# Delta-rule stage of a hybrid layer: GpSimd's two-tensor operations on other engines, and one convolution over context and tokens

## The chip, the core and the metric

The kernel runs on one core of a Trainium2 chip. A core has five engines that run side by side and meet at semaphores: PE (matrix products), DVE (VectorE, elementwise), ACT (ScalarE, function and copy), POOL (GpSimd) and SP, which issues DMAs. Each engine works its own instructions strictly in the order of the program. The metric is the device time of one execution in microseconds (us), as the median of repeated runs.

## The reference

One layer takes 512 latent tokens and 256 context tokens of width 1024. After modulated RMS norm, one projection feeds a bidirectional gated delta rule (8 heads of 128) and a latent attention (8 heads); their outputs are gated, merged, projected and followed by a squared-ReLU MLP. The change concerns the delta rule:

```python
def _centred_conv(x, w):                       # width 5, along the tokens; context and latents apart
    k_w = w.shape[0]; t = x.shape[1]; p = k_w // 2
    xp = jnp.pad(x, ((0, 0), (p, p), (0, 0)))
    return sum(xp[:, i:i + t] * w[i] for i in range(k_w))
# _gdn_inputs: qkv = silu(conv(qkv)); q, k = l2norm(q), l2norm(k); beta = sigmoid(..); g = -exp(a) * softplus(..)
a_mat = jnp.where(strict, einsum(kb, k) * decay, 0.0)
t_mat = triangular_solve(eye + a_mat, eye, lower=True, unit_diagonal=True)
u, w = t_mat @ vb, t_mat @ (kb * exp(gc))
def step(s, inp):                              # over the chunks, forwards and backwards
    v_new = u_i - w_i @ s
    o_i = qd_i @ s + qk_i @ v_new
    s = s * gl_i + kd_i.T @ v_new
```

## The kernel before, in words

Work is laid out with 128 rows on the partitions. The 256 context tokens are blocks 0 and 1, the 512 latent tokens blocks 2 to 5 of 128. Products run as three products of high and low parts (`mm3`), so each weight chunk that comes by DMA as `wf` is split by `wchunk` into `wh` (a cast on ScalarE, L180) and `wl` (a subtraction `wf - wh`, L181, on the engine `eng`). For the chunks of `w_qkv` (24 chunks of two pieces), `w_z` (8) and `w_gate` (16) `eng` is GpSimd, 96 pieces of 128x512 in all; elsewhere it is VectorE, or both in turn.

The delta rule takes two heads at a time (a pair), four pairs. For each pair:

- `gdn_in` projects k, v and q of both heads into PSUM. `convolve` copies each result to `raw` (ScalarE, L459), scales it by the middle tap (ScalarE, L461) and adds the four other taps on VectorE (L465), for the 512 latent columns and for the 256 context columns apart, then applies silu by a tanh on ScalarE (L469) and one VectorE instruction (L470).
- `gdn_gram` makes decays and Gram matrices for three double blocks. Four instructions of VectorE write the factor `Bt` (L571), GpSimd multiplies it by the decay `gam` (L573), VectorE by the Gram matrix in PSUM into `A` (L579). GpSimd cuts the triangles `rh` that feed the decay products (L555).
- `gdn_prep` inverts the 32x32 diagonal blocks by a loop of 60 dependent VectorE instructions on `pt` and `tu` (L614, L615; called the solve here), with a trip through DRAM before it (`dA`) and behind it (`dB`), and puts the blocks together by products with `off`, which is `A` masked by GpSimd to the neighbours of the diagonal blocks of 32 and then of 64 (L606), and with `S`, `S2`, `R`, `R2` (L635 to L653), three of whose products per pair are GpSimd's.
- `gdn_chain` walks the six blocks in both directions. Each step waits for the step before: `Em` and `Qm` (triangles, GpSimd, L710), `rho` (VectorE, L741), products, `y2` (VectorE, two instructions per direction, L756), `y` (ScalarE, L761), products, the state `s` (VectorE, L777).
- `gdn_out` norms and gates the output (`ob`, VectorE, L822).

The chunks of `w_z` and `w_gate` are written at low priority between pairs, to fill TensorE. The order on each engine is not written by hand: the program is given to a scheduler that fixes each engine's order before the run, from its own idea of how long things take. Two lines set what is done at one time:

```python
    prep1 = gdn_prep(1, ops1, gram1)
    ops2, gram2 = gdn_in(2)
    with low():
        fill(1)
    gdn_out(1, gdn_chain(1, ops1, prep1))
```

so the solve of one pair lies beside the projections and convolutions of the next and the chain of the one before. Latent attention and the MLP follow.

Of the kernel before, what the change touches and what calls it, by code (L numbers as in the profile page):

```python
# [7 lines left out]
F32 = mybir.dt.float32  # L8
# [7 lines left out]
P = 128  # L16
# [18 lines left out]
def _masks():  # L35
# [16 lines left out]
        "off32": (p // 64 == i // 64) & (p // 32 != i // 32),  # L52
        "off64": p // 64 != i // 64,
# [32 lines left out]
def tile_layer(ctx, tc, I, out, stop=None, dbg=None):  # L86
# [123 lines left out]
    def gemv_step(q, acc, kt, ws):  # L210
        """acc += silu(c) * rows of w_mod."""
# [46 lines left out]
    def spill(piece, b, po, tag):  # L258
        """normalised rows, transposed, to DRAM."""
# [24 lines left out]
    def rms(t, n, r, tag):  # L284
        """1 / rms over the channels, in every partition."""
# [128 lines left out]
    # rotated key part, shared by the heads  # L414
# [38 lines left out]
    def convolve(pl, pc, ch, dst, nctx):  # L453
        """dst (P, nctx + 512) = silu(conv)."""
        raw = gx.tile([P, NT], F32, tag="raw", name="raw")
        for src, o, L in ((pl, nctx, NL), (pc, 0, NC)):
            if src is None:
                continue
            act.copy(raw[:, o:o + L], src)  # L459
            src = raw[:, o:o + L]  # L460
            act.activation(dst[:, o:o + L], src, AF.Identity, scale=convh[:, ch, 2:3])  # L461
            for i in (0, 1, 3, 4):
                s = i - 2
                a, z = max(0, -s), L - max(0, s)
                dve.scalar_tensor_tensor(dst[:, o + a:o + z], src[:, a + s:z + s], convh[:, ch, i:i + 1],  # L465
                                         dst[:, o + a:o + z], ALU.mult, ALU.add)
        n = nctx + NL
        tt = raw[:, :n]
        act.activation(tt, dst, AF.Tanh)  # L469
        dve.scalar_tensor_tensor(dst, tt, 1.0, dst, ALU.add, ALU.mult)  # L470

    def transposes(src, nb, tag):
        """src (P, nb*128) -> list of (PSUM tile, first block, count)."""
        res = []
        b = 0
        while b < nb:
# [880 lines left out]
```

## Time and profile before

| | us |
|---|---|
| median of three executions | 1366.33 |
| the three executions | 1363.82, 1366.33, 1374.16 |
| profiled execution, span from the first to the last instruction | 1372.9 |
| busy in that span: PE, DVE, ACT, POOL | 1286.1, 907.8, 614.5, 423.8 |
| DVE busy from 125 to 640 us (delta rule) | 391 |

The profile's span is that of one execution; what lies around it is not in its rows. A busy PE counts overlapped ends of matmuls and is not PE at its peak. Of each group of instructions the profile gives busy time, mean length, and the idle time before it with what ended it. [...]

### The profile page before, as it was taken

To read this page: it belongs to the slowest core of one execution; us is meant where nothing else is said; L and a number is where in the kernel's file an instruction comes from. 1 tells how busy PE (TensorE), PEld (TensorE's weight loads), DVE (VectorE), ACT (ScalarE), POOL (GpSimd) and SP (SyncE) were. 2 spreads that over 40 slices of the span, in tenths; PEclk is the share of its full clock that TensorE was granted. 3 is DMA by queue.
4 is the path that set the end of the run, shared out by engine and by line. 5 is a ranking of instruction groups with operands and counts; after the bars stand their busy time and mean duration, and the time that the engine had idled before them with its cause. 6 is when DMAs were issued, how large, how long until landed. Compare 5 with 4: busy or idle time off the path is not lost.

```text
span 1372.9 us, 21048 instructions
## 1 busy us (share of the span) xinstructions
PE 1286.1 (94%) x7430; PEld 1124.4 (82%) x7430; DVE 907.8 (66%) x1925; ACT 614.5 (45%) x1562; POOL 423.8 (31%) x446
## 2 busy tenths in 40 slices
PE   5999887998998989898999999999999999999998
PEld 4897776797787978787888998888897888888887
DVE  4758798777877787846886887786877333333333
ACT  4555544336452635335565776523353233242331
POOL 0156557443653564441222221122123011010110
PEclk9999998999999999998999999999999999999999
DMA  9332213320233123324010101485734222222232
GB/s 365 99 121 80 56 54 91 94 70 1 93 109 92 31 78 109 100 84 145 7 51 12 38 32 69 167 300 164 267 112 165 88 98 93 100 93 99 93 104 96
DMA packets 97992, 141.33 MB, mean 103 GB/s; under 512 B 32736, under 2 KB 41824, under 8 KB 97760
## 3 DMA queue, kind: packets, MB, share of 16 engines
q1 hardware_dynamic: 68576, 127.41, 27.4%
q10 hardware_dynamic: 29312, 12.59, 3.7%
q8 instruction: 59, 0.97, 0.3%
q14 instruction: 45, 0.37, 0.1%
HBM read 124.36 MB, written 15.60 MB: 102 GB/s over the span
## 4 chain that ended last, share of the span: by engine, by line
PE 57%; DVE 15%; ACT 4%; DMA 3%; issue 2%; POOL 1%; ACTq 0%; SPq 0%; DVEq 0%; POOLq 0%
PE d L186 14%; PE d L188 13%; PE d L187 13%; DVE tu L614 2%; DVE vT L465 2%; DVE pt L615 2%; PE c L749 1%; PE p L1028 1%; PE c L734 1%; PE p L186 1%; PE p L187 1%; PE p L188 1%; PE c L769 1%; DVE pp L1018 1%; PE p L657 1%
## 5 line engine op out<-in xcount | busy, mean ns | idle before, releaser
L180 ACT CAST wh<-wf 128x512 fp32r<-128x512 f32 (+2 forms) x292 | 176.8, 610 | 382.3 <-PE d L187 260.6
L181 POOL TENSOR_TENSOR wl<-wf,wh 128x512 fp32r<-128x512 f32 x120 | 168.3, 1403 | 271.8 <-ACT wh L180 253.7
L181 DVE TENSOR_TENSOR wl<-wf,wh 128x512 fp32r<-128x512 f32 (+2 forms) x172 | 115.6, 677 | 121.0 <-ACT wh L180 119.8
L186 PE MATMUL d<-hTh,wh 128*128 128x512 f32 x384 | 158.7, 413 | 1.2 <-DVE tz L839 1.1
L187 PE MATMUL d<-hTl,wh 128*128 128x512 f32 x384 | 156.6, 408 | 0.0
L188 PE MATMUL d<-hTh,wl 128*128 128x512 f32 x384 | 155.6, 407 | 0.0
L1215 POOL TENSOR_TENSOR a<-r 128x512 f32<-128x512 f32 (+1 forms) x36 | 36.4, 1012 | 271.3 <-ACT r L1213 264.7
L186 PE MATMUL d<-ah,wh 128*128 128x512 f32 x256 | 100.7, 395 | 0.0
L187 PE MATMUL d<-al,wh 128*128 128x512 f32 x256 | 100.7, 395 | 0.0
L188 PE MATMUL d<-ah,wl 128*128 128x512 f32 x256 | 100.6, 395 | 0.0
L188 PE MATMUL d<-h2h,wl 128*128 128x512 f32 x224 | 87.4, 390 | 2.4 <-DVE wl L181 2.4
L186 PEld LDWEIGHTS d<-hTh,wh 128*128 128x128 f32 x384 | 75.6, 197 | 16.1 <-DVE tz L839 1.7
L188 PEld LDWEIGHTS d<-hTh,wl 128*128 128x128 f32 x384 | 75.3, 196 | 14.9
L187 PE MATMUL d<-h2l,wh 128*128 128x512 f32 x224 | 87.2, 389 | 0.0
L186 PE MATMUL d<-h2h,wh 128*128 128x512 f32 x224 | 87.2, 389 | 0.0
L187 PEld LDWEIGHTS d<-hTl,wh 128*128 128x128 f32 x384 | 75.5, 197 | 13.8
L1254 DVE SCALAR_TENSOR_TENSOR x<-d,mcol,x 128x512 f32<-128x512 f32 x32 | 24.0, 751 | 61.5 <-PE d L188 61.5
L614 DVE TENSOR_TENSOR tu<-pt 96x30 f32<-96x30 f32 (+14 forms) x120 | 52.9, 441 | 17.7 <-DMA pt<-dA 14.9
L188 PEld LDWEIGHTS d<-ah,wl 128*128 128x128 f32 x256 | 48.1, 188 | 11.6
L186 PEld LDWEIGHTS d<-ah,wh 128*128 128x128 f32 x256 | 48.1, 188 | 11.5
L187 PEld LDWEIGHTS d<-al,wh 128*128 128x128 f32 x256 | 48.1, 188 | 11.5
L615 DVE TENSOR_TENSOR pt<-pt,tu 96x30 f32<-96x30 f32 (+14 forms) x120 | 53.1, 442 | 2.8
(544 smaller groups left out, 3531.0 us busy)
## 6 DMA issues: line engine op xcount, KB each, us to landing
wf<-in_w_mi SPq DMA_DIRECT2D x64, 256.0 KB, 2.6
wf<-in_w_mo SPq DMA_DIRECT2D x64, 256.0 KB, 2.6
wf<-in_w_qkv SPq DMA_DIRECT2D x48, 256.0 KB, 2.7
wm<-in_w_mod SPq DMA_DIRECT2D x40, 256.0 KB, 5.4
wm<-in_w_mod SPq DMA_DIRECT2D x16, 512.0 KB, 9.1
wf<-in_w_gate SPq DMA_DIRECT2D x32, 256.0 KB, 2.6
wms<-in_w_mod SPq DMA_DIRECT2D x12, 512.0 KB, 8.2
wf<-in_w_z SPq DMA_DIRECT2D x16, 256.0 KB, 2.7
```

The source lines that it names most:

```text
L180: act.copy(wh, wf)
L181: eng.tensor_tensor(wl, wf, f32(wh), ALU.subtract)
L186: pe.matmul(po, lh, rh, start=first, stop=False)
L187: pe.matmul(po, lh, rl, start=False, stop=False)
L188: pe.matmul(po, ll, rh, start=False, stop=last)
L465: dve.scalar_tensor_tensor(dst[:, o + a:o + z], src[:, a + s:z + s], convh[:, ch, i:i + 1], dst[:, o + a:o + z], ALU.mult, ALU.add)
L614: dve.tensor_tensor(o, bc(pt[:, 0:k, k:k + 1], [96, k, w]), bc(pt[:, k:k + 1, k + 1:], [96, k, w]), ALU.mult)
L615: dve.tensor_tensor(pt[:, 0:k, k + 1:], pt[:, 0:k, k + 1:], o, ALU.add)
L657: pe.matmul(pv[:, c, :], off[:, c, :], R[:, c, :], start=True, stop=True)
L734: pe.matmul(t[:, 0, h, :], kT[:, h, 128 * bs[d]:128 * bs[d] + 128], S_[d][:, h, :], start=True, stop=True)
L1215: pool.tensor_tensor(a_, r, r, ALU.mult)
L1254: dve.scalar_tensor_tensor(x1[:, ot, :], po, mcol[:, 5, ot, 0:1], x1[:, ot, :], ALU.mult, ALU.add)
```

## The change

The code of the delta-rule stage is altered at these places; attention and MLP are as before but for the shape of one buffer.

- `wl` of `w_qkv`, `w_z` and `w_gate` is made by VectorE: 96 instructions change engine.
- `Bt` is written by ScalarE (48 instructions with a scale and a bias from memory), and its product with `gam` is VectorE's (12).
- The three products of `Dc` with the masks "up", "s2" and "s" are VectorE's (12).
- `off` is one lasting buffer. Instead of products with masks (24), GpSimd sets blocks to zero and copies blocks of `A`: per pair 2 memsets of 64 partitions, 4 copies of 32 partitions, 4 memsets of 32 partitions, 2 copies of 64.
- Of the two `y2` instructions of a step and direction one goes to ScalarE (40 of 80); the scaling of `ob` goes to ScalarE (32).
- `raw` is one lasting buffer with two zero columns before, between and behind context and tokens, so that each tap of k and v is one instruction over 770 columns, not two over about 512 and 256 (64 in place of 128), and ScalarE's scaling is one too. As the tanh overwrites the columns between, GpSimd sets them to zero again after each of the 16 convolutions. q keeps its 512 columns.

```diff
-    def convolve(pl, pc, ch, dst, nctx):
-        raw = gx.tile([P, NT], F32, tag="raw", name="raw")
-        for src, o, L in ((pl, nctx, NL), (pc, 0, NC)):
-            if src is None:
-                continue
-            act.copy(raw[:, o:o + L], src)
-            src = raw[:, o:o + L]
-            act.activation(dst[:, o:o + L], src, AF.Identity, scale=convh[:, ch, 2:3])
-            for i in (0, 1, 3, 4):
-                s = i - 2
-                a, z = max(0, -s), L - max(0, s)
-                dve.scalar_tensor_tensor(dst[:, o + a:o + z], src[:, a + s:z + s], convh[:, ch, i:i + 1],
-                                         dst[:, o + a:o + z], ALU.mult, ALU.add)
-        n = nctx + NL
-        tt = raw[:, :n]
+    GAP = 2
+    NG = NT + GAP
+    raw = gx.tile([P, NG + 2 * GAP], F32, name="raw")
+    pool.memset(raw[:, 0:GAP], 0.0)
+    pool.memset(raw[:, GAP + NC:GAP + NC + GAP], 0.0)
+    pool.memset(raw[:, NG + GAP:], 0.0)
+    def at(b):
+        return 128 * b + (GAP if b >= 2 else 0)
+    def convolve(pl, pc, ch, dst):
+        o = 0 if pc is not None else NC + GAP
+        n = NG - o
+        act.copy(raw[:, GAP + NC + GAP:GAP + NG], pl)
+        if pc is not None:
+            act.copy(raw[:, GAP:GAP + NC], pc)
+        act.activation(dst, raw[:, o + 2:o + 2 + n], AF.Identity, scale=convh[:, ch, 2:3])
+        for i in (0, 1, 3, 4):
+            dve.scalar_tensor_tensor(dst, raw[:, o + i:o + i + n], convh[:, ch, i:i + 1], dst, ALU.mult, ALU.add)
+        tt = raw[:, o + 2:o + 2 + n]
         act.activation(tt, dst, AF.Tanh)
         dve.scalar_tensor_tensor(dst, tt, 1.0, dst, ALU.add, ALU.mult)
+        if pc is not None:
+            pool.memset(raw[:, GAP + NC:GAP + NC + GAP], 0.0)
...
-            pl, pc = project(wchunk(I["w_qkv"][8 + hd], eng=pool), True)
+            pl, pc = project(wchunk(I["w_qkv"][8 + hd]), True)
...
+    off = gy.tile([P, 12, P], F32, name="off")
+    for c0 in range(0, 12, 4):
+        pool.memset(off[:, c0:c0 + 4, :], 0.0)
...
-                    dve.tensor_scalar(Bt[:, 2 * bb + h, :], f32(maskr[:, 1, :]), sA[:, b, 0, h:h + 1], sA[:, b, 1, h:h + 1],
-                                      op0=ALU.mult, op1=ALU.add)
-            pool.tensor_tensor(Bt, Bt, gam, ALU.mult)
+                    act.activation(Bt[:, 2 * bb + h, :], f32(maskr[:, 1, :]), AF.Identity,
+                                   scale=sA[:, b, 0, h:h + 1], bias=sA[:, b, 1, h:h + 1])
+            dve.tensor_tensor(Bt, Bt, gam, ALU.mult)
...
-        def masked(m):
-            t = gy.tile([P, 12, P], F32, tag="off", name="off")
-            for b2 in range(3):
-                cs = slice(4 * b2, 4 * b2 + 4)
-                pool.tensor_tensor(t[:, cs, :], A[:, cs, :], bc(M(m).unsqueeze(1), [P, 4, P]), ALU.mult)
-            return t
-        off = masked("off32")
+        def neighbours(n, fill):
+            for d in range(P // n):
+                q = slice(n * d, n * d + n)
+                e = slice(n * (d ^ 1), n * (d ^ 1) + n)
+                if fill:
+                    pool.tensor_copy(off[q, :, e], A[q, :, e])
+                else:
+                    pool.memset(off[q, :, e], 0.0)
+        neighbours(64, False)
+        neighbours(32, True)
...
-        pool.tensor_tensor(Dc, Dc, bc(M("up").unsqueeze(1), [P, 12, 32]), ALU.mult)
+        dve.tensor_tensor(Dc, Dc, bc(M("up").unsqueeze(1), [P, 12, 32]), ALU.mult)
...
-        expand(pool, S2, Dc)
+        expand(dve, S2, Dc)
         S = Dc
-        pool.tensor_tensor(S, Dc, bc(M("s").unsqueeze(1), [P, 12, 32]), ALU.mult)
+        dve.tensor_tensor(S, Dc, bc(M("s").unsqueeze(1), [P, 12, 32]), ALU.mult)
...
-        off2 = masked("off64")
+        neighbours(32, False)
+        neighbours(64, True)
...
-                    for h in HH:
-                        dve.tensor_scalar(t[:, h, :], p2[d][:, 0, h, :], bkd[:, bs[d], d, h:h + 1], None, op0=ALU.mult)
+                    dve.tensor_scalar(t[:, 0, :], p2[d][:, 0, 0, :], bkd[:, bs[d], d, 0:1], None, op0=ALU.mult)
+                    act.activation(t[:, 1, :], p2[d][:, 0, 1, :], AF.Copy, scale=bkd[:, bs[d], d, 1:2])
...
-                dve.tensor_scalar(ob[:, h, b, :], ob[:, h, b, :], so[:, h, b:b + 1], None, op0=ALU.mult)
+                act.activation(ob[:, h, b, :], ob[:, h, b, :], AF.Copy, scale=so[:, h, b:b + 1])
...
-        pz, _ = project(wchunk(I["w_gate"][i], eng=pool), False)
+        pz, _ = project(wchunk(I["w_gate"][i]), False)
...
-        pz, _ = project(wchunk(I["w_z"][hd], eng=pool), False)
+        pz, _ = project(wchunk(I["w_z"][hd]), False)
```

The scheduler then fixes another order. On VectorE, in the solve of the first pair, the rows before were these (`tu` and `pt` are the solve, `kT`, `vT` the convolution of the next pair):

```order
L614 TENSOR_TENSOR tu<-pt 96x234
L465 SCALAR_TENSOR_TENSOR vT<-raw,convh,vT 128x511
L465 SCALAR_TENSOR_TENSOR vT<-raw,convh,vT 128x254
L615 TENSOR_TENSOR pt<-pt,tu 96x18x13
L465 SCALAR_TENSOR_TENSOR vT<-raw,convh,vT 128x511
L465 SCALAR_TENSOR_TENSOR vT<-raw,convh,vT 128x255
L614 TENSOR_TENSOR tu<-pt 96x238
L465 SCALAR_TENSOR_TENSOR vT<-raw,convh,vT 128x510
L465 SCALAR_TENSOR_TENSOR vT<-raw,convh,vT 128x255
L615 TENSOR_TENSOR pt<-pt,tu 96x17x14
```

and at the same step of the solve they now are these (L629 and L630 are the solve, L474 ends a convolution, `br` are scalars of the next pair):

```order
L629 TENSOR_TENSOR tu<-pt 96x234
L510 TENSOR_SCALAR ssk<-ssk 128x6
L179 TENSOR_TENSOR wl<-wf,wh 128x512
L630 TENSOR_TENSOR pt<-pt,tu 96x18x13
L512 RECIPROCAL r_1916<-ssk 128x6
L474 SCALAR_TENSOR_TENSOR vT<-raw,vT 128x770
L629 TENSOR_TENSOR tu<-pt 96x238
L548 TENSOR_TENSOR br_2100<-beta,r_1916 128x24
L630 TENSOR_TENSOR pt<-pt,tu 96x17x14
L179 TENSOR_TENSOR wl<-wf,wh 128x512
```

The split convolution rows have moved away from this step, and two `wl` now stand between dependent rows of the solve.

On GpSimd, where the first pair's Gram matrices begin (`nk` is a power of six columns, `rh` triangles), the rows before were

```order
L181 TENSOR_TENSOR wl<-wf,wh 128x512
L151 TENSOR_TENSOR nk<-ssk,expt 128x6
L181 TENSOR_TENSOR wl<-wf,wh 128x512
L151 TENSOR_TENSOR nk<-ssk,expt 128x6
L181 TENSOR_TENSOR wl<-wf,wh 128x512
L573 TENSOR_TENSOR Bt<-Bt,gam 128x512
L181 TENSOR_TENSOR wl<-wf,wh 128x512
L606 TENSOR_TENSOR off<-A,mk 128x512
```

and now

```order
L149 TENSOR_TENSOR nk<-ssk,expt 128x6
L476 MEMSET raw 128x2
L536 MEMSET off 128x512 x3
L621 MEMSET off 64x12x64 x2
L149 TENSOR_TENSOR nk<-ssk,expt 128x6
L476 MEMSET raw 128x2
L566 AFFINE_SELECT rh<-ghi 128x256
L566 AFFINE_SELECT rh<-glo 128x256
L566 AFFINE_SELECT rh<-ghi 128x256
```

The `wl`, the product of `Bt` and the masked `off` are gone from here; memsets of `raw` and `off` stand in their place.

Later on GpSimd, where the first pair's blocks are put together and its chain begins (`Em`), the rows before were

```order
L573 TENSOR_TENSOR Bt<-Bt,QK 128x512
L647 TENSOR_TENSOR S_1831<-D_1801,mk 128x768
L181 TENSOR_TENSOR wl<-wf,wh 128x512 x2
L653 TENSOR_TENSOR D_1801<-D_1801,mk 128x384
L606 TENSOR_TENSOR off<-A,mk 128x512 x3
L181 TENSOR_TENSOR wl<-wf,wh 128x512 x5
L606 TENSOR_TENSOR off<-A,mk 128x512 x3
L181 TENSOR_TENSOR wl<-wf,wh 128x512
L710 AFFINE_SELECT Em<-A 128x256 x2
```

and now

```order
L631 MEMSET pt 96x32
L566 AFFINE_SELECT rh<-glo 128x256
L621 MEMSET off 32x12x32 x4
L619 COPY off<-A 64x12x64 x2
L621 MEMSET off 64x12x64 x2
L619 COPY off<-A 32x12x32 x4
L727 AFFINE_SELECT Em<-A 128x256 x4
```

Between the end of the solve and the first `Em`, memsets and copies stand where products and `wl` stood.

## Rows read from the trace of the kernel before

**Rows 1.** Windows of the delta-rule stage: busy us (instructions) per engine, granted clock, DMA.

```profile
core 0 of [0], span 1372.9 us
core 0: us, PE busy (x) PEld busy (x) DVE busy (x) ACT busy (x) POOL busy (x), PEclk, DMA share, GB/s
125.00:250.00 125.00, 105.36 (x560) 89.98 (x558) 101.13 (x180) 61.66 (x159) 78.96 (x82) 0.92 0.28 77
250.00:370.00 120.00, 109.97 (x709) 98.64 (x708) 98.98 (x228) 52.31 (x141) 59.19 (x72) 0.94 0.19 58
370.00:490.00 120.00, 116.23 (x706) 104.09 (x707) 91.90 (x217) 58.40 (x161) 60.85 (x69) 0.95 0.26 73
490.00:640.00 150.00, 135.67 (x746) 118.00 (x745) 99.31 (x221) 59.71 (x150) 67.23 (x75) 0.92 0.36 109
```

**Rows 2.** Chain that ended last, 259 to 640 us: share by line; then start, us, piece.

```profile
by line: PE d L186 6.9%; DVE tu L614 6.8%; DVE vT L465 6.8%; PE d L187 6.7%; PE d L188 6.7%; DVE pt L615 6.6%; issue 3.2%; PE c L749 2.8%; PE p L657 2.4%; DMA D<-dB 2.3%; PE c L734 2.3%; PE c L769 2.1%; PE p L691 2.0%; DMA dA<-DTa 1.9%; DMA
...
485.83 2.06 POOL Bt L573
```

**Rows 3.** Timeline of DVE and POOL, the third pair's solve: start us, us, engine, line.

```profile
401.02 0.96 DVE L614 TENSOR_TENSOR tu<-pt 96x30 f32<-96x30 f32 x1 [5.06 <-DMA pt<-dA]
...
407.36 0.55 POOL L710 TENSOR_SCALAR_AFFINE_SELECT Qm<-QK 128x256 f32<-128x256 f32 x1 [1.61 <-PE e L788]
407.68 0.43 DVE L614 TENSOR_TENSOR tu<-pt 96x184 f32<-96x184 f32 x1
408.15 0.34 DVE L615 TENSOR_TENSOR pt<-pt,tu 96x184 f32<-96x184 f32 x1
...
418.74 0.40 DVE L614 TENSOR_TENSOR tu<-pt 96x238 f32<-96x238 f32 x1
418.76 1.54 POOL L181 TENSOR_TENSOR wl<-wf,wh 128x512 fp32r<-128x512 f32 x1 [4.59 <-PE c L769]
419.18 1.39 DVE L615 TENSOR_TENSOR pt<-pt,tu 96x238 f32<-96x238 f32 x1
...
432.96 0.19 DVE L615 TENSOR_TENSOR pt<-pt,tu 96x30 f32<-96x30 f32 x1
```

**Rows 4.** One group of POOL, whole span: count | busy us, mean ns | idle before.

```profile
L181 POOL TENSOR_TENSOR wl<-wf,wh 128x512 fp32r<-128x512 f32 x120 | 168.3, 1403 | 271.8 <-ACT wh L180 253.7 <-PE c L769 7.0 <-issue 4.7
```

**Rows 5.** Groups of DVE, whole span, same columns.

```profile
L181 DVE TENSOR_TENSOR wl<-wf,wh 128x512 fp32r<-128x512 f32 (+2 forms) x172 | 115.6, 677 | 121.0 <-ACT wh L180 119.8 <-PE d L187 0.7
L614 DVE TENSOR_TENSOR tu<-pt 96x30 f32<-96x30 f32 (+14 forms) x120 | 52.9, 441 | 17.7 <-DMA pt<-dA 14.9
L615 DVE TENSOR_TENSOR pt<-pt,tu 96x30 f32<-96x30 f32 (+14 forms) x120 | 53.1, 442 | 2.8
L465 DVE SCALAR_TENSOR_TENSOR vT<-raw,convh,vT 128x510 f32<-128x510 f32 (+3 forms) x64 | 49.5, 814 | 4.0 <-ACT vT L461 3.7
L465 DVE SCALAR_TENSOR_TENSOR kT<-raw,convh,kT 128x510 f32<-128x510 f32 (+3 forms) x64 | 40.2, 671 | 9.4 <-ACT kT L461 9.0
L465 DVE SCALAR_TENSOR_TENSOR qT<-raw,convh,qT 128x510 f32<-128x510 f32 (+1 forms) x32 | 30.2, 944 | 7.5 <-ACT qT L461 7.0
L571 DVE TENSOR_SCALAR Bt<-maskr,sA 128x128 f32<-128x128 f32 x48 | 26.4, 613 | 0.1
L822 DVE TENSOR_SCALAR ob<-ob,so 128x128 f32<-128x128 f32 x32 | 11.8, 436 | 2.5 <-POOL so L151 2.3
L756 DVE TENSOR_SCALAR y<-c,bkd 128x128 f32<-128x128 f32 x80 | 23.7, 341 | 12.9 <-PE c L749 12.7
```

**Rows 6.** One line of DVE: count, ns min/median/max, first and last start.

```profile
L470 DVE SCALAR_TENSOR_TENSOR kT<-raw,kT x8: 943/958/1399, 96.8 to 471.2; 128x768 f32<-128x768 f32 x8
```

**Rows 7.** Groups of ACT, whole span, columns as in rows 4.

```profile
L761 ACT ACTIVATE y<-c,br 128x128 f32<-128x128 f32 x64 | 19.9, 367 | 40.7 <-DVE y L756 28.2 <-PE c L749 11.4 <-DMA dA<-DTa 0.9
L523 ACT ACTIVATE junk<-t 128x128 f32<-128x128 f32 x32 | 8.8, 276 | 2.6 <-PE t L480 1.1 <-ACT junk L523 0.5 <-ACT Da L586 0.4
```

**Rows 8.** Waits of POOL, 125 to 640 us: us in total, times, longest.

```profile
POOL wl L181 <- ACT wh L180: 97.0, 45, 7.9
```

More of the change, by code (lines that the diff above doesn't have):

```diff
@@ L479, in transposes @@
             for q in range(n):
-                pe.transpose(t[:, 128 * q:128 * q + 128], src[:, 128 * (b + q):128 * (b + q) + 128], ident)
+                c = at(b + q) if nb == 6 else 128 * (b + q)
+                pe.transpose(t[:, 128 * q:128 * q + 128], src[:, c:c + 128], ident)
             res.append((t, b, n))
@@ L485, in gdn_in @@
     def gdn_in(pr):
-        kT = gp.tile([P, 2, NT], F32, tag="kT", name="kT", bufs=2)
+        kT = gp.tile([P, 2, NG], F32, tag="kT", name="kT", bufs=2)
         qT = gp.tile([P, 2, NL], F32, tag="qT", name="qT", bufs=2)
@@ L496, in gdn_in @@
             hd = 2 * pr + h
-            pl, pc = project(wchunk(I["w_qkv"][8 + hd], eng=pool), True)
-            convolve(pl, pc, 8 + hd, kT[:, h, :], NC)
+            pl, pc = project(wchunk(I["w_qkv"][8 + hd]), True)
+            convolve(pl, pc, 8 + hd, kT[:, h, :])
             for t, b, n in transposes(kT[:, h, :], 6, "t"):
@@ L509, in gdn_in @@
             hd = 2 * pr + h
-            vT = gx.tile([P, NT], F32, tag="vT", name="vT")
-            pl, pc = project(wchunk(I["w_qkv"][16 + hd], eng=pool), True)
-            convolve(pl, pc, 16 + hd, vT, NC)
+            vT = gx.tile([P, NG], F32, tag="vT", name="vT")
+            pl, pc = project(wchunk(I["w_qkv"][16 + hd]), True)
+            convolve(pl, pc, 16 + hd, vT)
             for t, b, n in transposes(vT, 6, "t"):
@@ L518, in gdn_in @@
             hd = 2 * pr + h
-            pl, _ = project(wchunk(I["w_qkv"][hd], eng=pool), False)
-            convolve(pl, None, hd, qT[:, h, :], 0)
+            pl, _ = project(wchunk(I["w_qkv"][hd]), False)
+            convolve(pl, None, hd, qT[:, h, :])
             for t, b, n in transposes(qT[:, h, :], 4, "t"):
@@ L576, in gdn_gram @@
                 for h in range(2):
-                    s = kT[:, h, 128 * (2 * b2 + bb):128 * (2 * b2 + bb) + 128]
+                    s = kT[:, h, at(2 * b2 + bb):at(2 * b2 + bb) + 128]
                     pe.matmul(v4(pk)[:, 2 * bb + h, :], s, s, start=True, stop=True)
@@ L627, in gdn_prep @@
                     s = 128 * (2 * b2 + bb)
-                    pe.matmul(v4(pq)[:, 2 * bb + h, :], kT[:, h, s:s + 128], qT[:, h, s - NC:s - NC + 128],
+                    ks = at(2 * b2 + bb)
+                    pe.matmul(v4(pq)[:, 2 * bb + h, :], kT[:, h, ks:ks + 128], qT[:, h, s - NC:s - NC + 128],
                               start=True, stop=True)
@@ L680, in gdn_prep @@
         for c in range(12):
-            pe.matmul(pv2[c // 8][:, c % 8, :], off2[:, c, :], R2[:, c].rearrange("p e b -> p (e b)"),
+            pe.matmul(pv2[c // 8][:, c % 8, :], off[:, c, :], R2[:, c].rearrange("p e b -> p (e b)"),
                       start=True, stop=True)
@@ L733, in gdn_chain @@
                     for h in HH:
-                        pe.matmul(t[:, 0, h, :], kT[:, h, 128 * bs[d]:128 * bs[d] + 128], S_[d][:, h, :],
+                        pe.matmul(t[:, 0, h, :], kT[:, h, at(bs[d]):at(bs[d]) + 128], S_[d][:, h, :],
                                   start=True, stop=True)
@@ L1002, in attention @@
         for q2 in range(2):
-            pth = gp.tile([P, 6, 256], F32R, tag="kT", name="pth", bufs=2)
+            pth = gp.tile([P, 2 * NG], F32R, tag="kT", name="pth", bufs=2)[:, 0:1536]
+            pth = pth.rearrange("p (a b) -> p a b", a=6)
             ptl = gp.tile([P, 6, 256], F32R, tag="kn", name="ptl", bufs=2)
```

2 lines of the change are left out of this document (removed).

## The prediction

> **What bounds the kernel now.** I read the windows by stage first. [...] No engine is full, so I read the chain of waits next. From 259 to 640 us the three rows of `d` (TensorE's projections) hold 20.3% of it, and three VectorE rows alone (the two lines of the solve and the convolution of v) 20.2%, which is 77 us of 381 [rows 2]. The stage is a loop that passes through VectorE again and again, with GpSimd in it at places (a product `Bt` of 2.06 us [rows 2]).
>
> Then I looked at why VectorE's instructions are long, in the timeline of a solve. The reader is to see one pattern: the row `pt` of 238 columns starts at 419.18, while GpSimd's `wl` runs from 418.76 to 420.30, and takes 1.39 us; the equally wide row ahead of it, which began just ahead of that `wl`, takes 0.40 [rows 3]. A VectorE instruction with two tensors in SBUF is held until GpSimd's two-tensor instruction ends. GpSimd's triangle `Qm` (one tensor), 0.55 us from 407.36, leaves the first row of 184 columns at 0.43 where the next one, clear of it, takes 0.34 [rows 3]: a one-tensor instruction holds little.
>
> **The change part by part,** in VectorE's time within the stage.
>
> *Onto VectorE.* 96 `wl` at 0.68 [rows 5] are 65 us; 12 products of `Bt`, also 128x512, are 8; 12 products of 384 or 768 columns at about the same length are 8 (5 if all were as short as 0.4, 19 if all were as long as the 1.6 us of a held one). Sum +81.
>
> *Off VectorE.* The 48 rows of `Bt` (L571) were 26.4 us; of `ob` (L822), 11.8, three pairs of four fall in the stage, 9; of `y2` (L756), 23.7, half go, 12 [rows 5]. Sum -47.
>
> *Convolution.* k and v cost 40.2 + 49.5 = 90 us in 128 instructions [rows 5]. Now they are 64 of 770 columns; the nearest row is the 128x768 one of L470 with 0.94 at least and 0.96 in the median [rows 6], so I take 1.0 each, 64 us: -26, between -25 and -30. q keeps its 32 instructions, but their mean of 0.94 [rows 5] is as long as 768 columns take unheld, so they are held by 0.2 or more: -6.
>
> *Solves.* The four solves cost 53 + 53 = 106 us [rows 5]. The third one's 60 rows, the first and the last of them in [rows 3], sum to 24.9 us; six of them are held, two of which [rows 3] shows (0.96 and 1.39 us), and at their neighbours' length it would be 20.3. Four such solves are 81: -25. The same relief on the other two-tensor rows (L470 has 1.40 at most against 0.94 [rows 6]) I put at -4.
>
> *Copies.* 24 block copies read SBUF on GpSimd still. The trace has no copy there. If one holds like `Qm`, 0.1 us, they cost 2; if like `wl`, 1.0, they cost 24. They read one tensor, so I lean to the first, 0.3 each: +7. Memsets read nothing, and I put them at nothing; the time they need on GpSimd is covered by its 249 idle us of the stage [rows 1].
>
> Together 81 - 47 - 26 - 6 - 25 - 4 + 7 = -20 us of 391. The reader should note how little of this comes from the largest move: `wl` on VectorE costs 65 us, against holds of at most its 1.40 us on GpSimd [rows 4], which struck only where a two-tensor row met it. The gain is in the 47 that ScalarE takes and in the merged convolution.
>
> *Path alone.* `Bt` on the chain was four VectorE rows of 0.61 [rows 5] and a GpSimd product, 2.06 where it shows on the chain [rows 2]. On ScalarE a row with one scale from memory takes 0.367 and one without 0.276 [rows 7], so each such operand is 0.09 and `Bt` with two is 0.46: 4 x 0.46 + 0.68 = 2.5 against 4.5, 2 us for each of 12 blocks; I count a quarter on the path, -6. `y2` was two VectorE rows in line, 0.68; now one of 0.34 lies beside one of 0.37: 0.3 for each of 40, half on the path's side, half of those hidden, -3.
>
> *ScalarE* gains 48 x 0.46 + 32 x 0.37 + 40 x 0.37 = 49 us, less about 5 for the merged scaling: 232 to 276 of 515. Not a bound; what it costs, if its cover goes, is in the rivals.
>
> [...]
>
> [...]
>
> *The new queue.* On GpSimd, `wl` waited 97.0 us in 45 waits for ScalarE's cast [rows 8], with little behind it but triangles. Now these waits stand in VectorE's queue, and behind each stand the rows of a solve, a convolution or a chain, as the order shows. VectorE comes to a `wl` later than GpSimd did, so most of the 97 is over by then. I take 6 us, between 0 and 48.
>
> Sum on the path: -20 - 6 - 3 - 5 + 6 = -28 us. Here I take the 20, which is 88 added against 108 removed, as lying on the path wholly: solve and convolution, where the relief falls, are what the chain names most of VectorE [rows 2], and the `wl` stand between their rows. If both counted by VectorE's visible fifth of the chain, the 20 would be 4 (rival 2); if the relief counted wholly and half of the `wl` fitted into idle time, it would be 53 (rival 3). The profiled execution's span is 1372.9 us, 6.6 above the median of 1366.3, and would become 1345; the median becomes 1338.
>
> Attention and MLP, behind 640 us, keep their engines; the last `gdn_out` moves its 3 us there to ScalarE, and the rest is unchanged.
>
> **The rivals.**
>
> 1. *The queue takes it back* (slower). Mechanism: VectorE stands at a `wl` whose `wh` is not cast, because ScalarE, with 44 us more to do, is late, or because the buffer that the cast needs is still read by TensorE; the solve behind it stands too, TensorE then waits for the solve, and the next cast is later still. For: 97 us of such waits were there [rows 8], and 1 to 2 `wl` stand between dependent rows of the solve. Against: ScalarE has 283 idle us in the stage. Each of the 96 needs 0.29 us of waiting in front of the path to cancel the 28, and 0.44 to make the kernel 1% slower (42 us). With half of the 97 the sum is -34 + 48 = +14, 1380 us; with all of it, 1429.
>
> 2. *Nothing to be measured.* The relief falls where VectorE had slack, the added 81 us where the chain runs, and TensorE's filler chunks were covering the waits anyway. For: GpSimd's `wl` cost nothing wherever VectorE read PSUM or idled, and VectorE idles 124 us in the stage [rows 1]. By a fifth of it on the path, -20 becomes -4 and the sum -12: 1354, within 1%.
>
> 3. *More than the sum.* The scheduler knew nothing of the holds, so the order before fell behind its plan, and TensorE's idle time grew with it. [...] With half of the 65 us of `wl` in VectorE's idle time, it is 33 better, 1305. Against: the low-priority chunks are only 48 of the 96.
>
> 4. *The copies hold as long as `wl` did,* so that the change doesn't do what it says. Then 17 us are lost from the sum: 1355, which lies between the forecast and rival 2; I count it with rival 2.
>
> **How the numbers follow.** About 1%, 14 us, is what a measurement of this kernel can tell from no change. The forecast, 1318 to 1352, has 0.46. Rival 3, below 1318, 0.19, of which 0.09 lies below 1300. Rivals 2 and 4, 1353 to 1380, 0.22. Rival 1, above 1380, 0.13. So faster by over 1% is 0.46 + 0.19 = 0.65, within 1% 0.22, slower 0.13. The range goes from 1300 to 1376: it leaves out 0.09 below and some 0.14 above at most, of which the edge of rival 2 is a part, and reaches to the other cases for the rest. The likeliest case's own range is 1318 to 1352.
>
> **What would show each step.** In the profile after: `wl` of 128x512 on VectorE at 0.68 to 0.72, with no row of the solve above 0.6 but beside GpSimd's triangles and copies; the solve's two lines together at 80 to 88 us instead of 106; the 770-column rows at 0.96 to 1.02; `Bt` on ScalarE at 0.42 to 0.50; GpSimd's busy time in the stage under 150 us; VectorE's busy time from 125 us to the end of the stage at 360 to 380. The clock of the stage should rise to 0.95 or more. Rival 1 would show as VectorE's idle time in front of `wl`, put down to ScalarE's cast, of more than 30 us in the stage; rival 2 as VectorE's busy time down by 20 and its idle time up by as much; rival 4 as rows of the solve of 1 us beside copies. The forecast is wrong if VectorE's busy time in the stage does not fall, or if it falls and the stage still ends after 630 us.

## The result and the profile after

The changed kernel takes 1330.53 us in the median (1323.24 to 1335.15), the kernel before 1366.83 beside it: a ratio of 0.972, 95% interval 0.968 to 0.976. The forecast was 1338, with a range of 1300 to 1376. The total was near; the experiments show that it was near for a reason other than the sum's.

The profiled executions are 1372.9 and 1330.7 us long, 42.2 apart. The row of ScalarE that reads latent attention's first projection (`junk`, L930 before, L947 after) stands at 641.8 us before and at 606.4 after, so 35 of the 42 us lie ahead of it, in the delta-rule stage; most of the other 7 in attention, beside which the last pair's chain still runs; the MLP is as long as it was.

The windows of the stage after, the rows that answer to [rows 1] (columns as there, from 125 us to the end of the stage):

```profile
core 0: us, PE busy (x) PEld busy (x) DVE busy (x) ACT busy (x) POOL busy (x), PEclk, DMA share, GB/s
125.00:250.00 125.00, 116.42 (x620) 98.95 (x619) 102.94 (x199) 71.80 (x182) 41.38 (x60) 0.96 0.33 90
250.00:370.00 120.00, 110.99 (x726) 100.50 (x725) 87.08 (x193) 62.97 (x175) 40.41 (x72) 0.94 0.17 49
370.00:490.00 120.00, 117.89 (x740) 105.05 (x740) 93.98 (x211) 70.59 (x196) 34.81 (x57) 0.99 0.30 87
490.00:605.00 115.00, 110.88 (x643) 97.86 (x642) 79.72 (x197) 56.51 (x149) 20.15 (x36) 0.96 0.42 123
```

VectorE is busy 103 + 87 + 94 + 80 = 364 us (391 before), ScalarE 262 (232), GpSimd 137 (266), and the granted clock is 0.94 to 0.99 (0.92 to 0.95). TensorE is busy 456 of 480 us, before 467 of 515.

The chain of waits from 259 to 605 us, by line, against [rows 2]:

```profile
by line: PE d L184 15.9%; PE d L185 15.4%; PE d L186 15.1%; PE c L766 4.1%; PE c L786 3.8%; PE c L751 3.4%; PE e L802 3.3%; PE e L805 2.9%; DVE kT L471 2.0%; issue 1.9%; PE t L487 1.8%; PE p L683 1.7%; DMA sz<-d_z 1.7%; PE p L708 1.6%; PE p
```

TensorE's projections (`d`) had 20.3% and now have 46.4%; the solve's two lines and the convolution of v, which had 20.2%, are gone from the head of the list. Most of the chain is now TensorE's.

The groups of VectorE, ScalarE and GpSimd that answer to [rows 4 to 7], columns as there:

```profile
L179 DVE TENSOR_TENSOR wl<-wf,wh 128x512 fp32r<-128x512 f32 (+2 forms) x268 | 182.9, 686 | 164.2 <-ACT wh L178 161.5 <-PE d L186 1.4 <-PE d L185 0.7
L630 DVE TENSOR_TENSOR pt<-pt,tu 96x30 f32<-96x30 f32 (+14 forms) x120 | 41.7, 347 | 2.2
L629 DVE TENSOR_TENSOR tu<-pt 96x30 f32<-96x30 f32 (+14 forms) x120 | 41.6, 346 | 7.5 <-DMA pt<-dA 5.1
L471 DVE SCALAR_TENSOR_TENSOR vT<-raw,convh,vT 128x770 f32<-128x770 f32 x32 | 33.3, 1042 | 6.5 <-ACT vT L469 6.1
L471 DVE SCALAR_TENSOR_TENSOR kT<-raw,convh,kT 128x770 f32<-128x770 f32 x32 | 33.0, 1031 | 5.3 <-ACT kT L469 4.7
L471 DVE SCALAR_TENSOR_TENSOR qT<-raw,convh,qT 128x512 f32<-128x512 f32 x32 | 25.2, 787 | 4.3 <-POOL raw L476 3.1 <-ACT qT L469 0.7
L772 DVE TENSOR_SCALAR y<-c,bkd 128x128 f32<-128x128 f32 x40 | 13.6, 343 | 3.1 <-PE c L766 2.8
```

```profile
L582 ACT ACTIVATE Bt<-maskr,sA 128x128 f32<-128x128 f32 x48 | 19.6, 499 | 0.8 <-DVE sA L552 0.7
L773 ACT ACTIVATE y<-c,bkd 128x128 f32<-128x128 f32 x40 | 14.4, 369 | 33.8 <-DVE y L772 33.0 <-DVE wl L179 0.8
L839 ACT ACTIVATE ob<-ob,so 128x128 f32<-128x128 f32 x32 | 9.8, 388 | 0.9 <-POOL so L149 0.8
```

```profile
L619 POOL COPY off<-A 32x384 f32<-32x384 f32 (+1 forms) x24 | 19.1, 794 | 13.1 <-DVE A L590 12.1
L621 POOL MEMSET off<- 32x384 f32 (+1 forms) x24 | 12.5, 520 | 51.3 <-PE p L673 31.8 <-PE p L698 18.6
```

The solves take 41.7 + 41.6 = 83.3 us (106 before), the convolution of k and v 66.3 (89.7), q 25.2 (30.2). `wl` costs VectorE 0.69 us. What is left of [rows 8] now stands in VectorE's list of waits (us in total, times, longest; 125 to 605 us):

```profile
DVE wl L179 <- ACT wh L178: 23.8, 20, 4.3
```

### The profile page after: what moved, and what is told of

It reads as the page before. It is cut to its first block, busy times and chain, and to the rows that moved or that the text cites. A ratio compares the mean times of both kernels' runs of the same rounds, so it can differ in the third digit from the quotient of the medians.

```text
span 1330.7 us, 21029 instructions
## 1 busy us (share of the span) xinstructions
PE 1269.9 (95%) x7430; PEld 1112.8 (84%) x7430; DVE 867.2 (65%) x1861; ACT 648.2 (49%) x1666; POOL 278.5 (21%) x372
## 4 chain that ended last, share of the span: by engine, by line
PE 82%; DVE 7%; DMA 4%; ACT 4%; issue 1%; POOL 1%; SPq 0%; DVEq 0%; ACTq 0%; POOLq 0%
PE d L184 20%; PE d L185 20%; PE d L186 20%; DMA wm<-in_w_mod 2%; PE p L184 1%; PE c L766 1%; PE p L185 1%; PE p L186 1%; PE c L786 1%; PE p L1046 1%; PE c L751 1%; PE e L802 1%; DVE kT L471 1%; PE e L805 1%; PE t L487 1%
## 5 line engine op out<-in xcount | busy, mean ns | idle before, releaser
L179 DVE TENSOR_TENSOR wl<-wf,wh 128x512 fp32r<-128x512 f32 (+2 forms) x268 | 182.9, 686 | 164.2 <-ACT wh L178 161.5
L179 POOL TENSOR_TENSOR wl<-wf,wh 128x512 fp32r<-128x512 f32 x24 | 36.2, 1510 | 133.3 <-ACT wh L178 133.3
L186 PEld LDWEIGHTS d<-h2h,wl 128*128 128x128 f32 x224 | 42.0, 188 | 10.1 <-DVE wl L179 1.4
L184 PEld LDWEIGHTS d<-h2h,wh 128*128 128x128 f32 x224 | 42.0, 188 | 8.7
```

The source lines that it names most:

```text
L179: eng.tensor_tensor(wl, wf, f32(wh), ALU.subtract)
L184: pe.matmul(po, lh, rh, start=first, stop=False)
L186: pe.matmul(po, ll, rh, start=False, stop=last)
```

## The experiments

Three measures recur, all worked out from the trace. The **stage** runs from 125 us to the row `junk` of attention that the section above names. The **holds** are the sum, over VectorE's rows of the stage, of what each takes above the fastest tenth of its line and shape. **TensorE's loss** is read from the intervals from one matmul's start to the next: of an interval of 1.4 times the usual one of its shape (the lower quartile) or more, what it has above the usual counts as slow up to 2.1 times that, and as standing still beyond. What is left, TensorE's own work, is 422 to 429 us in all fourteen kernels. These two parts are good to some 2 us. The median is that of all executions, the other columns are those of the one that was profiled; it took 1374 us for the kernel before, and lay 9 us above the median for products and copies alone, 5.5 above for `wl` on VectorE in the order of before, and 6 below for `wl` on GpSimd in the new order.

| kernel | median us | stage | VectorE busy | holds | TensorE slow + still |
|---|---|---|---|---|---|
| before | 1369 | 517 | 392 | 78 | 40 + 51 |
| the change | 1331 | 481 | 364 | 18 | 26 + 28 |
| `wl` on VectorE alone | 1328 | 476 | 390 | 33 | 22 + 30 |
| the change without that | 1346 | 495 | 358 | 60 | 27 + 42 |
| convolution alone | 1370 | 517 | 385 | 76 | 41 + 47 |
| ScalarE moves alone | 1369 | 515 | 361 | 67 | 37 + 50 |
| products and copies alone | 1368 | 520 | 400 | 73 | 43 + 48 |
| `wl` on VectorE, order of before | 1356 | 506 | 394 | 33 | 41 + 41 |
| `wl` on GpSimd, new order | 1354 | 496 | 399 | 84 | 31 + 42 |
| one select for `wl`, order of before | 1331 | 477 | 354 | 41 | 24 + 27 |
| two selects for `wl`, order of before | 1347 | 493 | 368 | 54 | 30 + 37 |
| `wl` on VectorE + products and copies | 1341 | 485 | 393 | 21 | 25 + 33 |
| `wl` on VectorE + ScalarE moves | 1351 | 490 | 370 | 34 | 29 + 38 |
| the same, order of `wl` alone | 1331 | 483 | 366 | 29 | 24 + 34 |

The kernel before ran beside every group of runs, at 1367.9 to 1369.7 us.

The granted clock goes with the slow part. The traces before and after hold two values of it, 1 and 0.5. Of the stage TensorE had 0.5 for 72 us before (a mean of 0.93 over 517 us) and for 38 after the change, 31 with `wl` on VectorE alone, 72 with that in the order of before, 41 with `wl` on GpSimd in the new order, 31 with one select and 41 with two.

**One part at a time.** First the largest part alone (the same edit for the chunks of k, v, q, `w_gate` and `w_z`):

```diff
-            pl, pc = project(wchunk(I["w_qkv"][8 + hd], eng=pool), True)
+            pl, pc = project(wchunk(I["w_qkv"][8 + hd]), True)
```

> The kernel before with one part of the change alone: the 96 wl of w_qkv, w_z and w_gate on VectorE; GpSimd keeps its products and masks, the convolution stays in two pieces. Theory S (the sum of the prediction): 96 x 0.68 = 65 us come onto VectorE and some 35 us of holds go (solves 25, other rows 4, q 6), so VectorE has 30 us more to do in the stage and the kernel gets slower, 1380 to 1396 us. Rival H (the holds lie on the path, the added wl beside it): faster, 1335 to 1350, with VectorE's share of the chain in the stage well under the 140 us of before. Rival N: within 1%, the two cancel.

It took 1328.39 us, 0.971 (0.968 to 0.973): as much as the whole change, and 7 us below the range that H named. The window of its stage (columns as in [rows 1]):

```profile
125.00:600.60 475.60, 448.48 (x2713) 396.30 (x2712) 390.43 (x920) 229.73 (x607) 156.25 (x211) 0.97 0.29 88
```

VectorE is busy 390 us here, as long as before, in a stage that is 41 us shorter. So VectorE's load alone did not set the length of the stage.

The opposite, the changed kernel with `eng=pool` put back at the five places:

> The changed kernel with the 96 wl put back on GpSimd, all else as changed. S: 65 us leave VectorE and about 33 us of holds come back, so it beats the changed kernel by some 30 us: about 1300. H: the holds come back onto the path: 1350 or more, solve rows of 1.4 us beside wl, the clock of the stage at 0.95 or less. N (the changed kernel's stage is bound by TensorE, whose rows hold 365 of 480 us of its chain): within 13 us of 1331 either way.

It took 1346.28 us, 0.984 (0.981 to 0.987): slower than the changed kernel by 16 us, where the sum wanted it 30 faster, and between the ranges of N (up to 1344) and H (from 1350). Its solves, in the groups of VectorE:

```profile
L629 DVE TENSOR_TENSOR tu<-pt 96x30 f32<-96x30 f32 (+14 forms) x120 | 58.9, 491 | 8.3 <-DMA pt<-dA 5.3
L630 DVE TENSOR_TENSOR pt<-pt,tu 96x30 f32<-96x30 f32 (+14 forms) x120 | 50.0, 416 | 2.8
```

108.9 us, 3 more than before. The other three parts together, with the order that the scheduler gave them, are therefore worth something (1369 to 1346) while `wl` holds VectorE. One by one they are not. The merged convolution alone, by the edit of `convolve` that the change shows:

> The kernel before with the merged convolution alone. S: 64 rows of 770 columns instead of 128, 26 us less on VectorE, which the prediction took as path: about 1340. H: the longer rows meet GpSimd's wl as often as the short ones did, and a held row ends when the wl ends: 1355 to 1366, with held rows of 1.4 to 2 us among the 770-column ones. If the gain of the whole change is this part alone, the time is 1331 to 1335.

1370.00 us, ratio 1.001 (0.999 to 1.002): nothing gained, and 4 us above the range of H. The groups of VectorE:

```profile
L473 DVE SCALAR_TENSOR_TENSOR vT<-raw,convh,vT 128x770 f32<-128x770 f32 x32 | 39.0, 1218 | 13.4 <-ACT vT L471 12.8
L473 DVE SCALAR_TENSOR_TENSOR kT<-raw,convh,kT 128x770 f32<-128x770 f32 x32 | 34.4, 1075 | 14.5 <-ACT kT L471 13.8
```

The rows of k and v fell from 89.7 to 73.4 us and not to 66, since nearly a third of the saving goes into holds (1.22 us for a row of v that takes 1.04 in the changed kernel), and VectorE's idle time ahead of them, 13.4 us [rows 5], is 27.9. The moves to ScalarE alone:

```diff
-                    dve.tensor_scalar(Bt[:, 2 * bb + h, :], f32(maskr[:, 1, :]), sA[:, b, 0, h:h + 1], sA[:, b, 1, h:h + 1],
-                                      op0=ALU.mult, op1=ALU.add)
+                    act.activation(Bt[:, 2 * bb + h, :], f32(maskr[:, 1, :]), AF.Identity,
+                                   scale=sA[:, b, 0, h:h + 1], bias=sA[:, b, 1, h:h + 1])
...
-                dve.tensor_scalar(ob[:, h, b, :], ob[:, h, b, :], so[:, h, b:b + 1], None, op0=ALU.mult)
+                act.activation(ob[:, h, b, :], ob[:, h, b, :], AF.Copy, scale=so[:, h, b:b + 1])
```

> The kernel before with the moves to ScalarE alone: the 48 Bt rows, half of y2, the scaling of ob; the product of Bt with gam stays on GpSimd. S: 47 us off VectorE (26 + 9 + 12) and 9 on the path: 1315 to 1325 if all of it counts, and this would be more than the whole change brings. H: the rows moved were partly holds and partly beside the path; 1345 to 1360. N: within 1%.

1369.01 us, ratio 1.000 (0.998 to 1.002). The window of its stage, and the groups of VectorE:

```profile
125.00:639.60 514.60, 467.56 (x2748) 408.73 (x2747) 361.21 (x752) 261.66 (x714) 261.77 (x299) 0.94 0.28 81
```

```profile
L614 DVE TENSOR_TENSOR tu<-pt 96x30 f32<-96x30 f32 (+14 forms) x120 | 52.3, 436 | 11.8 <-DMA pt<-dA 9.1
L615 DVE TENSOR_TENSOR pt<-pt,tu 96x30 f32<-96x30 f32 (+14 forms) x120 | 56.7, 472 | 3.3
L465 DVE SCALAR_TENSOR_TENSOR vT<-raw,convh,vT 128x510 f32<-128x510 f32 (+3 forms) x64 | 48.8, 804 | 23.3 <-ACT vT L461 23.1
```

VectorE has 31 us less to do and the stage is 2 us shorter. The solves are still 109 us, and VectorE now idles 23.1 us in front of the convolution of v for ScalarE's row L461, where it idled 3.7 [rows 5]. The fourth part alone:

```diff
-        off = masked("off32")
+        neighbours(64, False)
+        neighbours(32, True)
...
-        expand(pool, S2, Dc)
+        expand(dve, S2, Dc)
```

> The kernel before with the fourth part of the change alone: GpSimd's masked products become block copies and memsets, and its products of Bt and Dc go to VectorE; wl stays on GpSimd. S: 16 us of products and 7 of copies come onto VectorE, some holds go: no gain, 1360 to 1375. H: of the 63 us by which GpSimd's two-tensor rows hold VectorE in the stage, the masks and products do about 15; with these gone, a part of the 23 us appears that the changed kernel with wl on GpSimd still gained (the convolution alone and the ScalarE moves alone brought nothing): 1345 to 1358.

1367.93 us, ratio 1.000 (0.998 to 1.003). Theory H missed here: it named 1345 to 1358. The holds fell by 5 us only, 78 to 73: `wl`, which is still on GpSimd, does most of them.

What follows: of the four parts one brings the whole gain by itself, and it is the one that the sum had as a loss; the other three bring nothing one by one, and 23 us together. But each edit also gives the scheduler another plan, so the next runs hold the order.

**The order held.** Edges without a semaphore tie each instruction to its neighbour on its engine, by a table of the order that another kernel had:

```diff
+                tc.add_manual_dep(ins[j], ins[i].name, info, reason="order")
...
         tile_layer(tc, aps, out)
+        _pin(tc, ORDER)
```

In the traces of the five runs that hold an order, every row but the ones that the edit moves stands where the table has it, on all five engines. The kernel before with the edges and no other edit was not timed. First `wl` on VectorE in that order:

> The kernel before with the 96 wl on VectorE, but every other instruction of every engine held in the order of the kernel before (edges between neighbours in program text, without a semaphore); only the place of the wl among VectorE's rows is the scheduler's. Theory H (what brings the gain is that wl leaves GpSimd, whatever the order): 1325 to 1340 us. Rival O (the gain is the scheduler's new order, since a shorter wl in its plan lets it write another one): 1355 to 1370. In between, each has a part.

1355.80 us, 0.991 (0.988 to 0.994), the lower edge of O's range; its nine executions spread from 1348.6 to 1363.0. The window of its stage, and what VectorE waited for in front of `wl` (columns as in [rows 8]):

```profile
125.00:631.10 506.10, 469.05 (x2719) 414.70 (x2718) 393.75 (x922) 230.77 (x607) 160.55 (x210) 0.93 0.28 82
```

```profile
DVE wl L181 <- ACT wh L180: 27.7, 24, 3.7
```

The granted clock is 0.93 here, as before, where the same edit in the new order has 0.97. Then the opposite corner, `wl` on GpSimd in the order of the 1328 us version:

> The opposite corner: the 96 wl on GpSimd, all other instructions held in the order that the scheduler gave the kernel with wl on VectorE (the one that took 1328). H: the gain is gone, 1355 to 1385, with VectorE held as before. O: 1325 to 1345.

1354.16 us, 0.989 (0.985 to 0.993). Its solves (VectorE's groups) are the longest of all, 115 us:

```profile
L614 DVE TENSOR_TENSOR tu<-pt 96x30 f32<-96x30 f32 (+14 forms) x120 | 55.6, 463 | 10.8 <-DMA pt<-dA 8.1
L615 DVE TENSOR_TENSOR pt<-pt,tu 96x30 f32<-96x30 f32 (+14 forms) x120 | 59.6, 497 | 2.7
```

Neither theory holds alone. The engine of `wl` is worth 14 us in the old order and 26 in the new one, the order 15 with `wl` on GpSimd and 27 with `wl` on VectorE. So of the 41 us that `wl` on VectorE brought in the scheduler's own order, 14 are the move in the old order and 27 are the order that came with it. In the profiled executions the two orders' stages differ by 21 and 30 us, and TensorE's slow part is 9 of the 21 and 19 of the 30: what the order changes is for a good part how long TensorE runs at half its clock.

Moving `wl` does two things at once: it frees VectorE of the holds and loads it with 60 us of `wl`. To part them, `wl` stays on GpSimd, in the old order, and reads one tensor:

```diff
-            eng.tensor_tensor(wl, wf, f32(wh), ALU.subtract)
+            eng.tensor_tensor(wl, wf, f32(wh), ALU.subtract) if eng else pool.affine_select(wl, f32(wh), pattern=[[1, step * n]], compare_op=ALU.is_ge, fill=0.0, base=0, channel_multiplier=1)
...
-            pl, pc = project(wchunk(I["w_qkv"][8 + hd], eng=pool), True)
+            pl, pc = project(wchunk(I["w_qkv"][8 + hd], eng=None), True)
```

> The kernel before in its own order on all five engines; the 96 wl stay on GpSimd in the same places of its queue and wait for the same cast, but each is a triangle select over wh alone (one tensor, 512 columns, all kept), so the low part of these weights is left out of the result and wl holds wh. Theory H in its narrow form (the holds of VectorE by GpSimd's two-tensor rows cost the time): 1325 to 1345, with solves of 20 to 21 us instead of 25 to 28. Rival Q (GpSimd's queue costs it: the selects and powers behind the wl, and the wl itself that comes late to TensorE): 1355 to 1370, since the queue is as long. The new row should take 1.0 to 1.2 us against 1.40, so up to a fifth of Q's cost may go too.

1331.31 us, 0.974 (0.970 to 0.978), the whole gain, with PE, DVE, ACT, POOL and SP in the order of before. Its solves took 90.9 us, 22.7 each, where 20 to 21 were expected (26.5 before). The select also lets go of `wf` as soon as the cast is done; that is not what gained, since ScalarE's cast waited only 1.9 us for a `wf` in the stage before. But the select is also half as long as the subtraction (GpSimd's groups):

```profile
L181 POOL TENSOR_SCALAR_AFFINE_SELECT wl<-wh 128x512 fp32r<-128x512 f32 x96 | 68.4, 713 | 146.4 <-ACT wh L180 141.0 <-PE e L788 3.7 <-PE d L188 1.6
```

0.71 us, not the 1.0 to 1.2 that I expected, so GpSimd's queue was shorter too. The next run takes that away, with two selects in a row:

```diff
+            eng.tensor_tensor(wl, wf, f32(wh), ALU.subtract) if eng else [pool.affine_select(wl, f32(s), pattern=[[1, step * n]], compare_op=ALU.is_ge, fill=0.0, base=0, channel_multiplier=1) for s in (wh, wl)]
```

> As the run with one triangle select in place of each wl, in the order of the kernel before on all five engines, but with two selects in a row for each wl (the first over wh, the second over wl in place): one select took 0.71 us, so two take 1.42, as long as the subtraction's 1.40, and each reads one tensor only. wl holds wh, so the low part of these weights is left out of the result. Narrow H (VectorE's holds cost the time, GpSimd's occupation does not): 1325 to 1345. Rival Q (the gain of the single select came from the 0.7 us by which GpSimd's queue and TensorE's wl were early): 1355 to 1370. In between, the difference to 1331 is Q's part and the difference to 1369 H's.

1347.19 us, 0.984 (0.981 to 0.986). GpSimd's groups and the window of the stage:

```profile
L181 POOL TENSOR_SCALAR_AFFINE_SELECT wl<-wh 128x512 fp32r<-128x512 f32 x96 | 67.7, 705 | 120.1 <-ACT wh L180 111.6 <-PE d L188 4.5 <-PE c L769 3.7
L181 POOL TENSOR_SCALAR_AFFINE_SELECT wl<-wl 128x512 fp32r<-128x512 f32 x96 | 65.7, 685 | 6.6
```

```profile
125.00:617.90 492.90, 458.11 (x2730) 404.75 (x2729) 367.81 (x843) 232.19 (x611) 264.50 (x379) 0.96 0.29 84
```

GpSimd is busy 264.5 us, as before (266), and the time is 22.5 us shorter than that of the kernel before. By the expectation's own split 22 us are H's and 16 Q's. The count of the holds, made after the run, says why that gives Q too much: the selects still hold VectorE a little, 0.1 to 0.2 us each, and twice as many hold more. In the one order, 78 us of holds give 1369, 54 give 1347 and 41 give 1331: 23 or 24 us of holds fewer are 22.5 us, with GpSimd as long busy as before, and 37 fewer are 38; in the profiled executions themselves the stage is 24 and 40 us shorter. In this order the time follows the holds, one for one. At that rate 13 of the 16 us between two selects and one are holds, and the 3 that GpSimd's queue may have had are too few for these runs. TensorE's slow part is 10 of the 24 us and 16 of the 40: a hold's price includes the clock.

**Is VectorE's load anything?** Two sums of parts, with the scheduler's own order. `wl` on VectorE with the products and copies:

> The kernel before with wl on VectorE and with the products and masks of GpSimd replaced as in the change; the convolution in two pieces and no move to ScalarE. If the changed kernel's stage is bound by TensorE and not by VectorE's load (H), then this is as fast as both, 1322 to 1334, though VectorE has some 65 us more to do than in the changed kernel. S: VectorE's 26 + 6 of convolution and 47 of ScalarE moves come back: 1355 or more.

1341.25 us, 0.979 (0.976 to 0.982), though its holds are 12 us less than those of `wl` alone: slower than H said and faster than S did. And `wl` on VectorE with the moves to ScalarE:

> The kernel before with wl on VectorE and with the moves to ScalarE, the rest as before. H: 1318 to 1332; if VectorE's load still counts a little where a solve or a chain has no other work beside it, this is the best of all, some 5 us below the version with wl alone (1328). S: 47 us less than the version with wl alone, 1285.

1350.73 us, 0.987 (0.984 to 0.990): 22 us slower than without them, which no theory had. The last run adds the same moves with the order of the 1328 us version held:

> The version with wl on VectorE alone (1328 us), its order held on all five engines, with the 120 moves to ScalarE (Bt, half of y2, ob) added; only the place of these 120 among ScalarE's rows is the scheduler's. With the scheduler's own order the same parts took 1351. Theory O2 (those 22 us were the order): 1315 to 1332, and below 1325 if VectorE's load still counts, so that it beats both the kernel before and the changed one. Theory A (the moves themselves cost, since ScalarE's rows now stand in front of what TensorE waits for): 1340 to 1355. S, with 47 us less on VectorE: 1285.

1330.78 us, 0.972 (0.970 to 0.975). So 20 of the 22 us were the order that the scheduler wrote. And with the order held, 24 us less work on VectorE (390 to 366) gain nothing that can be measured. VectorE waits 24.4 us for the cast in front of `wl` here, and 12.1 without the moves, so part of what is taken off comes back as waiting.

No version beats the change by more than the runs can tell: `wl` alone, the change, and the last run are within 2.4 us of each other. (One select is as fast, but leaves the low part of these weights out of the result.)

## Why the prediction was right, and where it was not

*What bounds the kernel.* The reading of the chain was right: VectorE's solve and convolution, lengthened by GpSimd's rows, were on the path. The pattern of [rows 3] is what the held order shows as a cause (1369 to 1347 and 1331 when selects take the place of the two-tensor `wl` and no other row moves). Of the 28 rows of the solves that began in a running `wl` before, 25 ended 0.05 to 0.34 us behind its end. The step that priced this pattern was mis-sized twice. First, the holds: I counted 25 + 4 + 6 = 35 us of them as relief, and the stage had 78 before and 18 after. I had left out those in `Bt` and `ob`, which I took off at their held length, and in the convolution of k and v. One line of VectorE before, against another (count, ns min/median/max, first and last start):

```profile
L571 DVE TENSOR_SCALAR Bt<-maskr,sA x48: 331/434/1443, 118.4 to 493.5; 128x128 f32<-128x128 f32 x48
```

```profile
L579 DVE TENSOR_TENSOR A<-e,Bt x12: 676/685/693, 122.0 to 522.2; 128x512 f32<-128x512 f32 x12
```

`Bt` reads one tensor in SBUF and took up to 1.44 us all the same, while `A` (L579), whose other input lies in PSUM, was never held. My sentence "two tensors in SBUF" was too narrow.

Second, **the step that failed**: "I take the 20 ... as lying on the path wholly", for load and relief alike. The runs part the two. A hold counts one us for one in the old order. VectorE's own load counts less: in the old order 45 us of holds went and about 60 us of `wl` came, and 14 us were gained. If those holds were worth their 45, the `wl` on VectorE took back about 31; this is an inference, and as VectorE then also waited 27.7 us for the cast in front of `wl`, it does not part load from waiting. In the new order, 52 us of holds went and 26 were gained. Adding the ScalarE moves changed nothing measurable, alone or with the new order held. So the largest move, "65 us, against holds", which the sum had as a loss of some 30, gained 14 to 26 us with an order held and 41 with the order that the scheduler then wrote, which the sum had no term for; and "The gain is in the 47 that ScalarE takes and in the merged convolution" was wrong: alone, neither moved the time measurably.

The -6 for `Bt` and the -3 for `y2` were also taken beside the 26 and 12 us of the same rows; with the 20 wholly on the path, they are in part counted twice.

*Why the total came out near.* VectorE's busy time fell as the terms said, by 27 us of 391 (forecast 20): solves -23 (forecast -25), convolution -23 (-26), q -5 (-6), `y2` -10 (-12). That this is near the 36 us gained is chance: `wl` alone leaves the busy time at 390 and gains 41.

*The clock.* The sum took 5 us for it, a term that no run shows; what the runs show is that TensorE's slow part fell from 40 to 26 us, so 14 of the gain, nearly three times the 5, and its standing still from 51 to 28, 23 more. Together that is 37 us; TensorE's own work is 2 us longer, and 35 are left for the stage: the same gain, seen from TensorE. The stage's granted clock is 0.96, where 0.95 or more was the sign.

*The new queue.* Forecast 6, sign of rival 1 at 30: VectorE waited 23.8 us in 20 waits for the cast, below the sign. Its price alone was not measured: versions with 12.1 and 24.4 us of it take 1328 and 1331.

*Copies.* Forecast 0.3 us each, between 0.1 and 1.0. In the timeline of the second solve after (start, us, engine, line):

```profile
256.95 0.39 DVE L629 TENSOR_TENSOR tu<-pt 96x228 f32<-96x228 f32 x1
257.02 2.50 POOL L619 COPY off<-A 32x384 f32<-32x384 f32 x3
257.38 0.58 DVE L630 TENSOR_TENSOR pt<-pt,tu 96x228 f32<-96x228 f32 x1
257.99 0.57 DVE L629 TENSOR_TENSOR tu<-pt 96x220 f32<-96x220 f32 x1
```

Beside the copies a solve row takes 0.58 where its neighbour takes 0.39. Over the stage the copies, of 0.71 to 0.97 us each in the mean, hold VectorE for 3.1 us, 0.13 each, near the lower bound; rival 4 is out.

*ScalarE* gained 30 us, not 44. `Bt` took 0.50 there (0.46 forecast), at the edge of the sign. The 770-column rows took 1.03 and 1.04, just above theirs (0.96 to 1.02).

*The rivals.* Rival 3 came nearest in mechanism: the relief counts more than the `wl`, and the order was part of the gain. Its reason for the order, a plan that knows nothing of holds, is not shown: with `wl` still on GpSimd the new order has more holds (84 us) and is 15 us faster. Its time of 1305 was too low. Four versions with 354 to 390 us of VectorE's work end between 1328 and 1331, which looks like a floor: TensorE's own 425 us and some 50 that it loses in each of them. No run shows that the 50 could not go. Rival 2 is out for the change, and right for three of its four parts taken singly. Rival 1 did not come.

*What stays open.* What it is in the new order that saves 15 to 27 us, and keeps TensorE longer at its full clock, was not found, nor how the 31 us split into VectorE's load and its waits, nor whether the three parts that bring nothing alone do so because of their orders; only the ScalarE moves were run with an order held. Of the changed kernel's own 36 us, 16 go when `wl` returns to GpSimd; how the other 20 divide between the three parts and the order was not measured.

## What to carry to other kernels

Where one engine's rows stretch another's, ask not how much work the stretched engine has but whether its stretched rows lie on the path: here, of 78 us of holds, the 37 that one select took away were worth 38 us, and 60 us of load added to VectorE, with its waits, cost about half of themselves. A sum of busy times can meet the total, with most of its terms about right, and still name the wrong part as the gain; two runs, one part alone and the change without it, tell. And where a scheduler writes the order, hold it before comparing two edits: its choice alone moved this kernel by 15 to 27 us, as much as the engine of `wl` did (14 to 26).

## What the runs showed of the hardware that I had not expected

- `Bt` (L571), a VectorE row that reads one tensor from SBUF and writes SBUF, was held by the two-tensor `wl` of GpSimd: ten such rows that began in a running `wl` took 1.17 us in the mean, against 0.33 at least. Two lines with an input in PSUM were not: six rows of `A` that began so took 0.69, as elsewhere, and nine of `rho` (L741) 0.34, as elsewhere.
- A triangle select of 128x512 on GpSimd took 0.71 us, half of a subtraction of the same shape (1.40). Some 84 of the 96 fall in the stage; they held VectorE 0.1 to 0.2 us each, and as many subtractions 0.5 us each (45 us of holds went with them in the old order).
- GpSimd's copy of a block of 32 partitions x 384 columns took 0.71 us, of 64 x 768 0.97; its memsets of the same blocks 0.41 and 0.74.
